# Weight-sum steps behind the MLP's tiles, two turns inside the embedding's products, and a shared last addition

## The chip, the cores and the metric

The kernel runs on one core of a Trainium2 chip. A core has several engines, each with its own instruction order that is fixed when the program is built: PE (TensorE, matrix products), DVE (VectorE), ACT (ScalarE), POOL (GpSimd) and SP (SyncE, which here issues most DMAs). An engine executes its instructions in that order; an instruction that waits for another engine or for a DMA holds up everything behind it on its engine. The metric is the device time of one execution in microseconds (us); lower is better.

## What is computed

The reference is a trunk of two layers over 512 tokens of width 1024. Each layer has a token mixer (Mamba-2 in the first, HGRN2 in the second), a layer norm, an MLP, a second layer norm and a gated embedding:

```python
h = layer_norm(DEEPNORM_ALPHA * x + mix, ln_g[i, 0], ln_b[i, 0])
h = layer_norm(DEEPNORM_ALPHA * h + sq_relu_mlp(h, mlp_w1[i], mlp_w2[i]), ln_g[i, 1], ln_b[i, 1])
x = h + jax.nn.sigmoid(h @ ple_w_gate[i]) * (p[i] @ ple_w_proj[i])

def sq_relu_mlp(h, w1, w2):
    a = jax.nn.relu(h @ w1)
    return (a * a) @ w2
```

All is float32. The MLP is 1024 to 4096 to 1024; `ple_w_gate` is 1024x1024 and `ple_w_proj` 256x1024.

## The kernel before

**Numbers in two halves.** A float32 operand is split into a high half (`hi`, a cast on ACT, L114 for weights) and a low half (`lo`, the difference on DVE, L116). A product is three matmuls, hi·hi, hi·lo and lo·hi, summed in a PSUM bank (`mm3`, L120 to L122). Weights stream in from memory through tiles `raw` or `r` and are split into tiles `whi` and `wlo`, six buffers of each, used again in turn.

**Seven products instead of eight.** Both the MLP's second product and the gate's product are done by 2x2 blocks with seven block products (Strassen-Winograd): p1 to p7. They need sums of blocks on both sides. On the activation side the blocks are named a11, a12, a22, s1, s2, s3, s4 (tiles `b8` and `blk`); on the weight side t1 to t4, made by `weight_sums`.

**The MLP** (`mlp_and_gate`) goes in four groups of 1024 hidden units. `hidden(g)` makes group g in eight tile steps ("T"): product, relu, square, and, after the fourth and the eighth, `half_blocks`, which forms one half of the seven blocks. Each block is written by `put`: a cast on ACT (L357), its difference on DVE (L358); the sums between them are L362 to L366. `block_product` multiplies the group by its part of w2 in seven steps ("Q"), one group behind. The order of steps is written out in `PERIODS`: eight T; then three times "TTQTQTQTQTQTQTQ"; then seven Q of the last group (g == 4), in the order p1, p7, p6, p4, p5, p2, p3. Each block product of 24 matmuls covers two halves c of 12 matmuls each, and the order of these on PE is the scheduler's. p1 and p6 share a pair of PSUM banks (`x`, tiles py0 and py1): p1's result must be added to `acc` (L471) before p6 adds more matmuls to the same bank and is added in its turn.

**Weight sums of the gate.** While the MLP runs, `sums_ahead` forms the gate's weight sums. For each of four pieces it loads four blocks into a `whi` and a `wlo` buffer (256 KB DMAs), does four additions (L405 to L410), and writes the four sums, twice two, each as a high half (cast L417 into `sg`, store L418) and a low half (difference L420 in place, store L425, both stores issued from ACT's queue) into the array `pre`. It is a generator of 20 steps, five for each piece; before the change one step is taken after each Q of the three mixed periods. What a step adds on DVE is placed behind the instruction in `marks["acc"]` (the last addition of a block product to `acc`), its low stores behind `marks["act"]` (the last relu).

**The gate and the embedding** follow. `turned(c)` transposes a 128-token row block of the normed `acc` on PE (L318, eight transposes into two banks, pt and pm), and ACT and DVE copy it out in halves (L308, L309) and whole (L324, L326). `proj(c, h)` is the embedding's product of six matmuls; `product` the gate's. turned(0) is issued in the MLP's last block product p3, after its last matmul; turned(1) between proj(0, 0) and proj(1, 0). `finish` multiplies the projection by the sigmoid (L611), adds it to `acc` (L612) and, in the last layer, stores it (L614). In the last layer's last call the projection comes in two halves of 256 columns.

The functions that the change touches, with the line numbers of the profile:

Of the kernel before, what the change touches and what calls it, by code (L numbers as in the profile page):

```python
# [11 lines left out]
AF = mybir.ActivationFunctionType  # L12
# [4 lines left out]
T = 512  # L17
# [15 lines left out]
SUMS = (60, 300, 300, 300)  # L33
# [8 lines left out]
def trunk(ctx: ExitStack, tc, a):  # L42
    nc = tc.nc
# [14 lines left out]
    uid, marks = [0], {}  # L58
# [8 lines left out]
    def f32(t):  # L67
        return t.bitcast(F32)
# [31 lines left out]
    def behind(ins):  # L100
        return nullcontext() if ins is None else tc.issue_after(ins.ins)
# [17 lines left out]
    def mm3(out, sh, sl, mh, ml, start, stop, **kw):  # L119
        nc.tensor.matmul(out, sh, mh, start=start, stop=False, **kw)  # L120
        nc.tensor.matmul(out, sh, ml, start=False, stop=False, **kw)  # L121
        marks["pe"] = nc.tensor.matmul(out, sl, mh, start=False, stop=stop, **kw)  # L122
# [25 lines left out]
    acc = mk(accp, [P, NCH, D], "acc")  # L148
# [10 lines left out]
    with tc.high_priority(offset=FIRST):  # L159
# [190 lines left out]
    def half_blocks(blk, z0, z1, p):  # L350

        ks = slice(2 * p, 2 * p + 2)
        a11, a12, a21, a22 = z0[:, :, 256:], z1[:, :, 256:], z0[:, :, :256], z1[:, :, :256]

        def put(name, f):
            hi, lo = blk[name][:, 0, ks, :], blk[name][:, 1, ks, :]
            nc.scalar.copy(hi, f)  # L357
            nc.vector.tensor_sub(lo, f, f32(hi))  # L358

        put("a11", a11)  # L360
        put("a22", a22)
        nc.vector.tensor_add(a22, a21, a22)  # L362
        put("a12", a12)
        nc.vector.tensor_sub(a21, a11, a21)
        nc.vector.tensor_sub(a11, a22, a11)
        nc.vector.tensor_sub(a12, a12, a11)  # L366
        put("s2", a11)
        put("s3", a21)
        put("s1", a22)
        put("s4", a12)  # L370
# [65 lines left out]
            us.append((hi, lo))  # L436
        return us

    def block_product(w, blk, lead, first, after=None, turns=None, sums=None):
# [8 lines left out]
        def product(x, f, name, start, i, j, turns=None):  # L448
            us = [split(v) if f in (t1, t2, t3, t4) else unit(v) for v in f]
            if start:  # L450
                banks[name] = [bank(psy, "py%d" % c) if name == "x" else bank(psj, "pj") for c in range(2)]
            t = blk[x]
            for c in range(2):
                ps = banks[name][c]
                sl = slice(c * P, (c + 1) * P)
                for k in range(4):
                    hi, lo = us[k // 2]
                    ks = slice((k % 2) * 512, (k % 2 + 1) * 512)
                    w_ = hi[:, ks], lo[:, ks]
                    mm3(ps, t[:, 0, k, sl], t[:, 1, k, sl], *w_, start and k == 0, k == 3, skip_group_check=True)  # L460
                    if turns and (c, k) == (1, 3):
                        with behind(marks["pe"]):
                            turns()
                d = acc[:, 2 - 2 * i + c, j * 512 : (j + 1) * 512]
                with tc.high_priority(offset=SOON if after else 0):
                    if after and f in (w[1][0], t1, t4, w[1][1]):
                        marks["acc"] = nc.vector.tensor_tensor_reduce(
                            d, ps, d, 1.0, 0.0, ALU.add, ALU.add, sums[:, 2 - 2 * i + c, j : j + 1]
                        )
                    elif (i, j) in seen:  # L470
                        marks["acc"] = nc.vector.tensor_add(d, ps, d)  # L471
# [10 lines left out]
        p3 = lambda: product("s4", w[1][1], "x", False, 0, 1, turns)  # L482
        for f in (p1, p7, p6, p4, p5, p2, p3) if after else (p1, p2, p6, p7, p5, p4, p3):
            f()
            if after and f is p5:
                after(0), after(1)
            if after and f is p3:
                after(2), after(3)
            yield

    def mlp_and_gate(layer, h_s, last, turns=()):

        w1, w2 = a[f"w1_{layer}"], a[f"w2_{layer}"]
        blocks = {}
# [45 lines left out]
        for g, period in enumerate(PERIODS):  # L540
            if g < 4:
                tiles = hidden(g)
            if g > 0:
                if g == 4:
                    blk, after, turned, sums, later = norm_blocks(2 * layer + 1)
                    p_s = (mk(w4, [P, 2, T], "a", F32R), mk(w4, [P, 2, T], "b", F32R))
                    praw = mk(raws, [P, 1024], "raw")
                    nc.sync.dma_start(praw, a[f"pT_{layer}"].rearrange("p k t -> p (k t)"))
                    praw = praw.rearrange("p (k t) -> p k t", k=2)
                    nc.scalar.copy(p_s[0], praw)  # L550
                    nc.vector.tensor_sub(p_s[1], praw, f32(p_s[0]))
                w = [[[w2[8 * g - 8 + 4 * i + 2 * j + u] for u in range(2)] for j in range(2)] for i in range(2)]
                products = block_product(w, blocks.pop(g - 1), SUMS[g - 1], g == 1, *((after, lambda: turned(0), sums) if g == 4 else ()))
            for op in period:
                next(tiles if op == "T" else products)
                if 0 < g < 4 and op == "Q":
                    next(ahead, None)
                if g == 4:
                    for _ in ahead:
                        pass  # L560
# [14 lines left out]

        pus, pps, held = {}, {}, {}

        def proj(c, h, parts=1):
            if h not in pus:
                pus[h] = unit(a[f"wp_{layer}"][h])  # L580
            pu = pus[h]
            pps[c, h] = []
            n = 512 // parts
            for i in range(parts):
                pp = bank(psj, "pj")[:, :n]
                for k in range(2):
                    ks = slice(k * 512 + i * n, k * 512 + (i + 1) * n)
                    mm3(pp, p_s[0][:, k, c * P : (c + 1) * P], p_s[1][:, k, c * P : (c + 1) * P], pu[0][:, ks], pu[1][:, ks], k == 0, k == 1)
                pps[c, h].append(pp)

        def product(x, f, c, ps, start, hook=()):
# [10 lines left out]
        def finish(c, h, sg):  # L602
            with behind(marks["pe"]):
                while late:
                    late.pop(0)()
            pp = pps.pop((c, h))
            n = 512 // len(pp)
            for i, part in enumerate(pp):
                cs = slice(i * n, (i + 1) * n)
                d = acc[:, c, h * 512 + i * n : h * 512 + (i + 1) * n]  # L610
                nc.vector.tensor_mul(sg[:, cs], part, sg[:, cs])  # L611
                nc.vector.tensor_add(d, sg[:, cs], d)  # L612
                if last:
                    nc.sync.dma_start(a["out"][c * P : (c + 1) * P, h * 512 + i * n : h * 512 + (i + 1) * n], d)  # L614
            if not last:
                late.append(lambda: turn(h, c))

        two = lambda p, tag: [bank(p, tag % c if "%" in tag else tag) for c in range(2)]
        proj(0, 0)
        with behind(marks["pe"]):  # L620
            turned(1)
        proj(1, 0)
        xb = two(psy, "py%d")
        f = [unit(v) for v in wb[0][0]]
        for c in range(2):
# [12 lines left out]
        f = ready(pre, 2)  # L638
# [9 lines left out]
        f = ready(pre, 1)  # L648
# [4 lines left out]
        f = ready(pre, 3)  # L653
# [14 lines left out]
        for c in range(2):  # L668
            if c == 0:
                proj(0, 1)  # L670
            product("s4", f, c, xb[c], False)
            sg = tmp("sg", [P, T])
            nc.scalar.activation(sg, xb[c], AF.Sigmoid)
            if c:
                proj(1, 1, 2 if last else 1)
            finish(c, 1, sg)
        return x_n, late

# [811 lines left out]
```

## Time and profile before

| | |
|---|---|
| time, median of 3 runs | 1411.1 us (1411.07 to 1411.56) |
| the profiled execution's own time | 1411.54 us |
| its span, first to last instruction | 1409.8 us |
| granted TensorE clock, mean | 1.000 |
| matmuls | 7973 |
| DVE busy | 1076.0 us (76%) |
| ACT busy | 777.6 us (55%) |

A row of the timeline has start, duration, engine, source line, operation, output<-input, and in brackets the idle time of the engine just before it with the releaser that the profile infers. "PE a L1 <- ACT b L2: 3.1, 2, 1.8" in the list of waits means that the line L1 on PE waited for L2 on ACT 3.1 us in total, in 2 places, 1.8 us at the longest. The releaser is inferred from the last semaphore event the profile can see, so it can name a neighbour of the real one. Matmuls overlap: a 128x512 matmul is listed with some 0.39 us, but they start 0.23 us apart.

### The profile page before, as it was taken

What the parts mean: (1) busy time and instruction counts of PE and PEld (TensorE: products, weight loads), DVE (VectorE), ACT (ScalarE), POOL (GpSimd) and SP (SyncE); (2) the same over time, 40 slices, a digit from 0 to 9 for tenths busy, and PEclk for the clock granted to TensorE, in tenths of its full rate; (3) what the DMA queues carried; (4) which work ended last, traced back from release to release, by engine and by line L of the source; (5) the groups of instructions that cost most, each with busy time, mean ns of one, the idle gap of its engine ahead of it and who ended that gap; (6) DMA issues with size and microseconds to landing.
All of it is one profiled execution on the core that took longest, in us unless ns stands there. A gap on an engine that the chain in (4) does not pass through costs nothing.

```text
span 1409.8 us, 20492 instructions
## 1 busy us (share of the span) xinstructions
PE 1400.4 (99%) x7973; PEld 1168.9 (83%) x7973; DVE 1076.0 (76%) x1777; ACT 777.6 (55%) x1164; POOL 1.8 (0%) x11
## 2 busy tenths in 40 slices
PE   9999999999999999999999999999999999999998
PEld 7888888888988888887888888888898888888787
DVE  7997877696866878787985774776785877868986
ACT  7886666573554555545564446465454554544563
POOL 0000000000000000000000000000000000000000
PEclk9999999999999999999999999999999999999999
DMA  8423333323354646655473321222163566565364
GB/s 295 157 98 135 103 108 120 105 90 105 129 185 143 228 161 204 211 176 177 139 280 122 104 92 62 89 92 75 61 239 122 171 209 214 175 215 194 108 246 154
DMA packets 66819, 214.70 MB, mean 152 GB/s; under 512 B 7713, under 2 KB 8353, under 8 KB 66593
## 3 DMA queue, kind: packets, MB, share of 16 engines
q1 hardware_dynamic: 57504, 196.59, 41.6%
q10 hardware_dynamic: 9216, 16.78, 3.3%
q8 instruction: 63, 1.03, 0.3%
q14 instruction: 36, 0.29, 0.1%
HBM read 194.41 MB, written 18.94 MB: 151 GB/s over the span
## 4 chain that ended last, share of the span: by engine, by line
PE 96%; DMA 1%; DVE 1%; ACT 1%; issue 1%; SPq 0%; DVEq 0%; ACTq 0%
PE pj L120 25%; PE pj L122 24%; PE pj L121 24%; PE py L120 5%; PE py L122 5%; PE py L121 5%; PE py L881 1%; PE py L1147 1%; PE py L883 1%; DVE wlo L116 1%; PE pt L864 0%; DMA raw<-in_whvg 0%; DMA acc<-in_xw 0%; ACT whi L114 0%; DMA pre<-whi 0%
## 5 line engine op out<-in xcount | busy, mean ns | idle before, releaser
L116 DVE TENSOR_TENSOR wlo<-raw,whi 128x1024 fp32r<-128x1024 f32 x222 | 269.4, 1221 | 171.6 <-ACT whi L114 170.4
L114 ACT CAST whi<-raw 128x1024 fp32r<-128x1024 f32 x222 | 232.8, 1051 | 302.3 <-PE pj L121 157.5
L120 PE MATMUL pj<-b,whi 128*128 128x512 f32 (+1 forms) x1000 | 379.6, 380 | 0.0
L121 PE MATMUL pj<-b,whi 128*128 128x512 f32 (+1 forms) x1000 | 377.3, 377 | 0.0
L122 PE MATMUL pj<-b,wlo 128*128 128x512 f32 (+1 forms) x1000 | 377.3, 377 | 0.0
L122 PEld LDWEIGHTS pj<-b,wlo 128*128 128x128 f32 x1000 | 188.2, 188 | 34.8
L121 PEld LDWEIGHTS pj<-b,whi 128*128 128x128 f32 x1000 | 188.2, 188 | 34.2
L120 PEld LDWEIGHTS pj<-b,whi 128*128 128x128 f32 x1000 | 188.0, 188 | 34.1
L122 PE MATMUL pj<-whi,b 128*128 128x512 f32 x530 | 206.1, 389 | 0.0
L120 PE MATMUL pj<-whi,b 128*128 128x512 f32 x496 | 196.1, 396 | 0.0
L121 PE MATMUL pj<-wlo,b 128*128 128x512 f32 x496 | 193.2, 390 | 0.0
L114 ACT CAST whi<-r 128x1024 fp32r<-128x1024 f32 x64 | 67.2, 1053 | 96.6 <-PE pj L121 79.9
L122 PEld LDWEIGHTS pj<-whi,b 128*128 128x128 f32 x530 | 99.5, 188 | 20.7 <-DVE b L1342 0.2
L120 PEld LDWEIGHTS pj<-whi,b 128*128 128x128 f32 x496 | 93.2, 188 | 20.3 <-ACT k L1076 0.5
L121 PEld LDWEIGHTS pj<-wlo,b 128*128 128x128 f32 x496 | 93.2, 188 | 18.5
L120 PE MATMUL py<-whi,b 128*128 128x512 f32 x256 | 100.7, 393 | 3.1 <-ACT b L357 3.1
L122 PE MATMUL py<-whi,b 128*128 128x512 f32 x256 | 99.8, 390 | 0.0
L121 PE MATMUL py<-wlo,b 128*128 128x512 f32 x256 | 99.7, 389 | 0.0
L116 DVE TENSOR_TENSOR wlo<-r,whi 128x1024 fp32r<-128x1024 f32 x64 | 77.8, 1220 | 27.8 <-ACT whi L114 24.0
L120 PEld LDWEIGHTS py<-whi,b 128*128 128x128 f32 x256 | 48.0, 188 | 15.0 <-ACT b L357 3.9
L122 PEld LDWEIGHTS py<-whi,b 128*128 128x128 f32 x256 | 48.1, 188 | 10.1
L121 PEld LDWEIGHTS py<-wlo,b 128*128 128x128 f32 x256 | 48.1, 188 | 9.7
(374 smaller groups left out, 1934.1 us busy)
## 6 DMA issues: line engine op xcount, KB each, us to landing
raw<-in_w SPq DMA_DIRECT2D x112, 512.0 KB, 3.4
r<-in_w SPq DMA_DIRECT2D x64, 512.0 KB, 4.0
raw<-in_wssd SPq DMA_DIRECT2D x38, 512.0 KB, 3.6
a<-csd SPq DMA_DIRECT2D x16, 512.0 KB, 3.6
raw<-in_wso SPq DMA_DIRECT2D x16, 512.0 KB, 3.7
pre<-sg ACTq DMA_DIRECT2D x32, 256.0 KB, 3.0
whi<-pre SPq DMA_DIRECT2D x16, 512.0 KB, 5.3
wlo<-pre SPq DMA_DIRECT2D x16, 512.0 KB, 6.6
```

The costliest lines, as they stand in the source:

```text
L114: nc.scalar.copy(hi[:, :n], f)
L116: nc.vector.tensor_sub(lo[:, :n], f, f32(hi[:, :n]))
L120: nc.tensor.matmul(out, sh, mh, start=start, stop=False, **kw)
L121: nc.tensor.matmul(out, sh, ml, start=False, stop=False, **kw)
L122: marks["pe"] = nc.tensor.matmul(out, sl, mh, start=False, stop=stop, **kw)
L881: nc.tensor.matmul(yd[64 * r : 64 * r + 64, sl], xdt[:, c, r, :], m[:, r, sl], start=True, stop=c == 0)
L883: nc.tensor.matmul(yd[64 * r : 64 * r + 64, sl], pv[:, c - 1, r, :], ecs[:, r, (c - 1) * P : c * P], start=False, stop=True,)
L1147: nc.tensor.matmul(ps[r][32 * b : 32 * b + 32, base + n * c : base + n * c + n], kk[r][:, ts], moving(r, 4 * c + b), start=True, stop=True,)
```

## The change

Four edits:

- `sums_ahead` is advanced after each T step of the mixed periods instead of each Q step, and `half_blocks`' differences (L358) now also set `marks["acc"]`, so a step's DVE work is placed behind the last of either kind.
- turned(0) goes from behind p3's last matmul to behind the third matmul of proj(0, 0), and turned(1) from between the two projections to behind the third matmul of proj(1, 0).
- The last sigmoid of the last layer is done in two halves of 256 columns.
- Where `finish` works in two halves (only that last call), the addition of the first half goes from DVE to GpSimd.

```diff
         def put(name, f):
...
-            nc.vector.tensor_sub(lo, f, f32(hi))
+            marks["acc"] = nc.vector.tensor_sub(lo, f, f32(hi))
...
-                    if turns and (c, k) == (1, 3):
-                        with behind(marks["pe"]):
-                            turns()
...
-                products = block_product(w, blocks.pop(g - 1), SUMS[g - 1], g == 1, *((after, lambda: turned(0), sums) if g == 4 else ()))
+                products = block_product(w, blocks.pop(g - 1), SUMS[g - 1], g == 1, *((after, sums) if g == 4 else ()))
             for op in period:
                 next(tiles if op == "T" else products)
-                if 0 < g < 4 and op == "Q":
+                if 0 < g < 4 and op == "T":
                     next(ahead, None)
...
+                    if turn == c and k == 0:
+                        with behind(marks["pe"]):
+                            turned(c)
...
-                nc.vector.tensor_add(d, sg[:, cs], d)
+                (nc.vector if i == len(pp) - 1 else nc.gpsimd).tensor_add(d, sg[:, cs], d)
...
-        proj(0, 0)
-        with behind(marks["pe"]):
-            turned(1)
-        proj(1, 0)
+        proj(0, 0, turn=0)
+        proj(1, 0, turn=1)
...
-            nc.scalar.activation(sg, xb[c], AF.Sigmoid)
+            parts = 2 if last and c else 1
+            for i in range(parts):
+                cs = slice(i * 512 // parts, (i + 1) * 512 // parts)
+                nc.scalar.activation(sg[:, cs], xb[c][:, cs], AF.Sigmoid)
             if c:
-                proj(1, 1, 2 if last else 1)
+                proj(1, 1, parts)
```

**Place 1: DVE at the hand-over from the fourth group to the last block product, first layer.** A row is line, operation, output<-input with the tiles' numbers, and size. L358 and L362 to L366 are the last call of `half_blocks`; L420 the last low halves of the sums; L471 (L468 in the changed file) the additions of block products to `acc`. wlo_946 is a half of t2, the weight of p6; py0_935 the bank that p1 and p6 share. Before:

```order
L420 TENSOR_TENSOR whi_859_5154<-whi_859_5154,sg_899_5462 128x512
L420 TENSOR_TENSOR wlo_860_5155<-wlo_860_5155,sg_900_5466 128x512
L116 TENSOR_TENSOR wlo_938_5642<-r_922_5578,whi_937_5640 128x1024
L471 TENSOR_TENSOR acc_1_94<-py0_842_5041,acc_1_94 128x512
L116 TENSOR_TENSOR wlo_940_5646<-r_925_5587,whi_939_5644 128x1024
L116 TENSOR_TENSOR wlo_944_5678<-r_923_5581,whi_943_5676 128x1024
L358 TENSOR_TENSOR blk_818_4938<-b_846_5079,blk_818_4938 128x512
L116 TENSOR_TENSOR wlo_946_5682<-r_926_5590,whi_945_5680 128x1024
L358 TENSOR_TENSOR b8_814_4934<-b_890_5393,b8_814_4934 128x512
L358 TENSOR_TENSOR b8_813_4933<-b_890_5393,b8_813_4933 128x512
L362 TENSOR_TENSOR b_890_5393<-a_869_5247,b_890_5393 128x2x256
L471 TENSOR_TENSOR acc_1_94<-py0_935_5612,acc_1_94 128x512
```

and with the change:

```order
L358 TENSOR_TENSOR blk_822_4956<-b_848_5091,blk_822_4956 128x512
L420 TENSOR_TENSOR whi_808_4906<-whi_808_4906,sg_867_5225 128x512
L420 TENSOR_TENSOR wlo_809_4907<-wlo_809_4907,sg_868_5229 128x512
L116 TENSOR_TENSOR wlo_944_5678<-r_923_5581,whi_943_5676 128x1024
L365 TENSOR_TENSOR a_873_5267<-b_892_5405,a_873_5267 128x2x256
L358 TENSOR_TENSOR blk_821_4955<-a_873_5267,blk_821_4955 128x512
L366 TENSOR_TENSOR b_892_5405<-b_892_5405,a_873_5267 128x2x256
L358 TENSOR_TENSOR b8_820_4954<-a_873_5267,b8_820_4954 128x512
L116 TENSOR_TENSOR wlo_946_5682<-r_926_5590,whi_945_5680 128x1024
L358 TENSOR_TENSOR b8_819_4953<-b_892_5405,b8_819_4953 128x512
L358 TENSOR_TENSOR blk_822_4956<-b_892_5405,blk_822_4956 128x512
L468 TENSOR_TENSOR acc_1_94<-py0_935_5612,acc_1_94 128x512
```

The two L420 stood ahead of the splits and of the half-block chain, and now stand inside that chain, ahead of p6's split wlo_946 and of the addition on py0_935. That addition followed L362; now eight half-block rows, three splits and the two L420 stand between, and two more splits (wlo_948, wlo_950) follow it, ahead of the addition on p1's other bank.

**The same place on ACT.** L528 is the relu, L530 the square, L425 the stores of the last low sums; with the change relu and square have just gone by. Before:

```order
L528 ACTIVATE b_890_5393<-pj_901_5470 128x512
L425 DMA pre_0<-whi_859_5154 128x512
L530 ACTIVATE b_890_5393<-b_890_5393 128x1024
L425 DMA pre_0<-wlo_860_5155 128x512
L114 CAST whi_939_5644<-r_925_5587 128x1024
L114 CAST whi_943_5676<-r_923_5581 128x1024
L357 CAST blk_818_4938<-b_846_5079 128x512
L114 CAST whi_945_5680<-r_926_5590 128x1024
L357 CAST b8_814_4934<-b_890_5393 128x512
L357 CAST b8_813_4933<-b_890_5393 128x512
```

and with the change:

```order
L357 CAST b8_818_4952<-b_892_5405 128x512
L357 CAST b8_817_4951<-b_892_5405 128x512
L114 CAST whi_939_5644<-r_925_5587 128x1024
L357 CAST b8_819_4953<-b_892_5405 128x512
L357 CAST blk_822_4956<-b_848_5091 128x512
L114 CAST whi_943_5676<-r_923_5581 128x1024
L357 CAST blk_821_4955<-a_873_5267 128x512
L425 DMA pre_0<-whi_808_4906 128x512
L425 DMA pre_0<-wlo_809_4907 128x512
L357 CAST b8_820_4954<-a_873_5267 128x512
L114 CAST whi_945_5680<-r_926_5590 128x1024
L357 CAST blk_822_4956<-b_892_5405 128x512
```

The stores stood ahead of the square and of all casts; they now stand behind the square and the casts of a22, a12, s1 and s3 (b8_818, b8_817, b8_819, blk_821), ahead of that of s2 (b8_820) and ahead of the cast for whi_945. The buffer read by the store "pre<-whi" was the one that whi_939 takes next; now it is the one that whi_945 takes.

**Place 2: PE at the two turns, first layer.** pj_1002 and pj_1005 are proj(0, 0) and proj(1, 0) before (pj_1000 and pj_1003 with the change), L318 the transposes. Before:

```order
L318 MATMUL pt_981_5883<-cst_17_160,acc_1_94 128x128 x4
L318 MATMUL pm_982_5884<-cst_17_160,acc_1_94 128x128 x4
L120 MATMUL pj_1002_5938<-whi_1000_5934,a_918_5570 128x512
L121 MATMUL pj_1002_5938<-wlo_1001_5936,a_918_5570 128x512
L122 MATMUL pj_1002_5938<-whi_1000_5934,b_919_5571 128x512
L120 MATMUL pj_1002_5938<-whi_1000_5934,a_918_5570 128x512
L121 MATMUL pj_1002_5938<-wlo_1001_5936,a_918_5570 128x512
L122 MATMUL pj_1002_5938<-whi_1000_5934,b_919_5571 128x512
L120 MATMUL pj_1005_5961<-whi_1000_5934,a_918_5570 128x512
L121 MATMUL pj_1005_5961<-wlo_1001_5936,a_918_5570 128x512
L122 MATMUL pj_1005_5961<-whi_1000_5934,b_919_5571 128x512
L318 MATMUL pt_1003_5945<-cst_17_160,acc_1_94 128x128 x4
```

and with the change:

```order
L120 MATMUL pj_1000_5922<-whi_998_5918,a_918_5570 128x512
L121 MATMUL pj_1000_5922<-wlo_999_5920,a_918_5570 128x512
L122 MATMUL pj_1000_5922<-whi_998_5918,b_919_5571 128x512
L318 MATMUL pt_1001_5926<-cst_17_160,acc_1_94 128x128 x4
L318 MATMUL pm_1002_5927<-cst_17_160,acc_1_94 128x128 x4
L120 MATMUL pj_1000_5922<-whi_998_5918,a_918_5570 128x512
L121 MATMUL pj_1000_5922<-wlo_999_5920,a_918_5570 128x512
L122 MATMUL pj_1000_5922<-whi_998_5918,b_919_5571 128x512
L120 MATMUL pj_1003_5945<-whi_998_5918,a_918_5570 128x512
L121 MATMUL pj_1003_5945<-wlo_999_5920,a_918_5570 128x512
L122 MATMUL pj_1003_5945<-whi_998_5918,b_919_5571 128x512
L120 MATMUL pj_1003_5945<-whi_998_5918,a_918_5570 128x512
```

turned(0), which stood in front of proj(0, 0), stands three matmuls into it; turned(1)'s first four transposes (pt), which stood three matmuls into proj(1, 0), follow its last matmul, three rows behind the last one shown.

On the g = 4 hand-over PE's order differs too: before, six of p6's matmuls stood between the two halves of p7; with the change all 24 matmuls of p7 come ahead of the first of p6. At the program's end GpSimd has two more rows, L612 ISA and L612 TENSOR_TENSOR (128x256), the first behind its last memset, and DVE's last three are L611, L611 and L612 instead of L611, L612, L611, L612.

More of the change, by code (lines that the diff above doesn't have):

```diff
@@ L437, in ready, with block_product @@
         return us
-    def block_product(w, blk, lead, first, after=None, turns=None, sums=None):
+    def block_product(w, blk, lead, first, after=None, sums=None):
         with behind(marks.pop(("turned", 0), None) if first else None):
@@ L446, in block_product, with product @@
         banks = {}
-        def product(x, f, name, start, i, j, turns=None):
+        def product(x, f, name, start, i, j):
             us = [split(v) if f in (t1, t2, t3, t4) else unit(v) for v in f]
@@ L481, in block_product @@
         p4 = lambda: product("a22", t4, "y", False, 1, 0)
-        p3 = lambda: product("s4", w[1][1], "x", False, 0, 1, turns)
+        p3 = lambda: product("s4", w[1][1], "x", False, 0, 1)
         for f in (p1, p7, p6, p4, p5, p2, p3) if after else (p1, p2, p6, p7, p5, p4, p3):
@@ L576, in mlp_and_gate, with proj @@
         pus, pps, held = {}, {}, {}
-        def proj(c, h, parts=1):
+        def proj(c, h, parts=1, turn=None):
             if h not in pus:
```

## The prediction

> **What bounds the kernel now.** I read the first and the fourth part of the page, then PE's waits, then the time around the longest of them on ACT, DVE and PE.
>
> ```profile
> span 1409.8 us, 20492 instructions
> PE 1400.4 (99%) x7973; PEld 1168.9 (83%) x7973; DVE 1076.0 (76%) x1777; ACT 777.6 (55%) x1164; POOL 1.8 (0%) x11
> PE 96%; DMA 1%; DVE 1%; ACT 1%; issue 1%; SPq 0%; DVEq 0%; ACTq 0%
> ...
> PE py L120 <- ACT b L357: 3.1, 2, 1.8
> PE pm L155 <- DVE y L152: 1.1, 1, 1.1
> PE py L120 <- ACT whi L174: 0.7, 2, 0.5
> PE pt L318 <- ACT b L324: 0.3, 1, 0.3
> ```
>
> PE is busy for 99% of the span, and the change takes no matmul away. So it can gain only the waits that it touches: 3.1 us at L357 (once in each layer), 0.3 us at L324, and what follows the last matmul. The L152 and L174 waits lie where nothing is edited. The profiled execution took 1411.54 us, 1.7 us more than its span and 0.44 us over the median 1411.1; I add differences to the median.
>
> The 3.1 us stand where the fourth MLP group hands over to the last block product. In the first layer, the order of the columns being start, duration, engine, line, operation:
>
> ```profile
> 654.14 0.69 DVE L420 TENSOR_TENSOR whi<-whi,sg 128x512 fp32r<-128x512 f32 x1
> 654.86 0.33 ACTq L425 DMA_DIRECT2D pre<-whi  x1
> 655.98 1.06 ACT L530 ACTIVATE b<-b 128x1024 f32<-128x1024 f32 x1
> 658.96 2.00 ACT L114 CAST whi<-r 128x1024 fp32r<-128x1024 f32 x2 [1.92 <-DMA pre<-whi]
> 662.33 1.14 ACT L357 CAST b<-b 128x512 fp32r<-128x512 f32 x2
> 665.26 0.68 DVE L362 TENSOR_TENSOR b<-a,b 128x512 f32<-128x512 f32 x1
> 665.87 0.68 DVE L471 TENSOR_TENSOR acc<-py,acc 128x512 f32<-128x512 f32 x1
> 665.08 0.39 PE L122 MATMUL pj<-whi,blk 128*128 128x512 f32 x1
> 666.70 0.47 PE L120 MATMUL py<-whi,b 128*128 128x512 f32 x1 [1.23 <-ACT b L357]
> ```
>
> The last pair of pieces of the weight sums (L420) is stored by a DMA issued at 654.86. The tile that this DMA reads is the next buffer for a weight split, so ACT's cast L114 stands until 658.96. Behind it in ACT's order stand the two half-block casts L357, whose input (the square, L530) was ready at 657.04 but which run at 662.33. DVE's halves follow, then L362, then the addition L471 that reads bank py0; it ends at 666.55, and PE's 666.70 starts s2 (p6) in that bank. The profile names ACT L357, but that had been done since 663.47: the last releaser is DVE's L471.
>
> **The change: sums.** Advanced after each tile step, the 20 steps end earlier in the program. That takes the DMA out from in front of that cast. But the last step comes behind the half-block lows (marks["acc"] is now set there too), and the orders of the change show where: DVE's two last L420 stand inside the last half-block chain, and ACT's L425 behind the casts of s1 and s3, ahead of the cast for whi_945. That cast refills the buffer which the DMA reads. On DVE the split of wlo_946 needs this cast, and the addition on py0_935, which p6 waits for, stands three rows behind this split. The wait for the landing is moved, not removed.
>
> I work the queue out by hand, from rows of before. First the anchors and the pitches:
>
> ```profile
> 658.28 0.39 PE L122 MATMUL py<-whi,blk 128*128 128x512 f32 x1
> 659.87 0.39 PE L120 MATMUL py<-whi,b 128*128 128x512 f32 x1
> 662.59 0.39 PE L120 MATMUL pj<-whi,blk 128*128 128x512 f32 x1
> 672.55 0.50 PE L120 MATMUL py<-whi,b 128*128 128x512 f32 x1
> ...
> 660.04 2.36 DVE L116 TENSOR_TENSOR wlo<-r,whi 128x1024 fp32r<-128x1024 f32 x2 [2.00 <-PE py L122]
> 664.06 1.29 DVE L358 TENSOR_TENSOR b<-b,b 128x512 fp32r<-128x512 f32 x2
> ...
> 1307.44 4.07 DMA pre<-whi
> pre<-whi ACTq DMA_DIRECT2D x16, 256.0 KB, 3.8
> ```
>
> Twelve matmuls take 662.59 − 659.87 = 2.72 us. On DVE one 128x512 operation follows another after 0.60 us and lasts 0.69 (L358 x2: 1.29, each 0.69 long). Two L116 take 2.36, so the next operation follows one after some 1.13, by the same overlap of 0.09. Two of ACT's big casts take 2.00, one alone 1.05 (as at 1307.93 below, of the same size).
>
> - ACT: the square ends at 657.04, the two casts L357 at 658.2. The cast for whi_939 needs the matmul of 658.28 done: 658.71 to 659.76. So the two casts do come five microseconds sooner than the 662.33 of before.
> - DVE from 659.80 in its new order: L116 to 660.93, L364, L358 at 661.53, L420 at 662.13 to 662.82, L420 at 662.73, L116 at 663.33, L365 at 664.46, L358 at 665.06, L366 at 665.67, L358 at 666.27 to 666.95.
> - The store is issued when the first L420 ends, 662.85. With 3.8 us (the median of its 16) it lands at 666.65. ACT casts whi_945 until 667.70; DVE's L116 starts at 667.74, two L358 at 668.87 and 669.47, and the addition on py0_935 runs 670.07 to 670.75. p6 can start at 670.80.
> - PE, in its new order, runs all 24 matmuls of p7 first, so it gets to p6 at 662.59 + 5.44 = 668.03. It stands 2.77 us there. Then 12 matmuls, and the next bank's addition behind two more L116 (670.67 + 2.26 + 0.69 = 673.62): p1's second half starts at 673.65.
>
> In both kernels the same 48 matmuls lie between 659.87 and p1's second half, and without a wait it would start at 670.75. Before started it at 672.55, so 1.80 us were lost; now 2.90. Layer 0: **+1.1 us**.
>
> The second layer repeats this, 651.95 us later by its first p1 matmul and its square:
>
> ```profile
> 1307.93 1.06 ACT L530 ACTIVATE b<-b 128x1024 f32<-128x1024 f32 x1
> 1311.82 0.39 PE L120 MATMUL py<-whi,b 128*128 128x512 f32 x1
> 1319.27 0.47 PE L120 MATMUL py<-whi,b 128*128 128x512 f32 x1 [1.84 <-ACT b L357]
> 1325.12 0.50 PE L120 MATMUL py<-whi,b 128*128 128x512 f32 x1
> ```
>
> Here 1325.12 − (1311.82 + 10.88) = 2.42 us were lost before; with the same 2.90 now, **+0.5 us**. Together +1.6.
>
> The landing time is the unknown. From 666.87 − 1.05 − 662.85 = 2.97 us downwards it no longer matters, for DVE then gets to this L116 at 666.87 anyway, and the addition ends at 669.88: 0.87 us less in each layer, a sum of −0.2. Each microsecond of landing above 3.8 costs one in each layer: at the 4.07 of the chain's row +2.1. I take 3.8, since it is the same transfer.
>
> [...]
>
> In groups one to three the sums steps come behind tile steps instead of products. PE's order there is unchanged, and its waits above name nothing of those groups; the same DVE and ACT operations are only moved between products. I take 0. If that cover failed, a late split would cost one DVE operation of 0.6 to 1.2 us per place; DVE at 76% of the span leaves room for that.
>
> **The two turns.** Transposes of turned(0) and turned(1) go three matmuls (0.68 us) later. Around the second turn, before:
>
> ```profile
> 701.92 1.05 ACT L114 CAST whi<-raw 128x1024 fp32r<-128x1024 f32 x1 [0.58 <-DMA raw<-in_wg]
> 702.88 0.58 ACT L324 COPY b<-pt 128x512 f32<-128x512 f32 x1
> 702.85 0.40 PE L122 MATMUL pj<-whi,b 128*128 128x512 f32 x1
> 703.51 0.66 PE L318 MATMUL pt<-cst,acc 128*128 128x128 f32 x4 [0.26 <-ACT b L324]
> ```
>
> PE could have begun at 702.85 + 0.23 = 703.08 and began at 703.51, when L324 had emptied bank pt. L324 ran behind the cast of 701.92, which waited for a load and not for the turn. If cast and copy stay there, PE now asks at 703.76 and finds the bank free: −0.43. If all of it shifts with the transposes, 0. I take **−0.3**, nearer the first, as the cast's load has no tie to the turn. The second layer has no such wait.
>
> **The tail.** Columns as above:
>
> ```profile
> 1404.75 0.28 PE L122 MATMUL pj<-whi,b 128*128 128x256 f32 x1
> ...
> 1405.47 0.28 PE L122 MATMUL pj<-whi,b 128*128 128x256 f32 x1
> 1405.14 0.42 DVE L611 TENSOR_TENSOR sg<-pj,sg 128x256 f32<-128x256 f32 x1 [1.46 <-PE pj L122]
> 1405.95 0.42 DVE L611 TENSOR_TENSOR sg<-pj,sg 128x256 f32<-128x256 f32 x1
> 1406.40 0.43 DVE L612 TENSOR_TENSOR acc<-sg,acc 128x256 f32<-128x256 f32 x1
> 1404.36 0.60 ACT L673 ACTIVATE sg<-py 128x512 f32<-128x512 f32 x1 [2.12 <-PE py L122]
> 729.09 0.99 POOL L1009 MEMSET sc<- 128x512 f32 x2 [387.66 <-DVE b L309]
> ```
>
> The sigmoid ends at 1404.96, before DVE's first product at 1405.14, which waited for PE; its halves gain nothing. Without the first addition DVE's second product starts when PE's last matmul is out, 1405.47 + 0.28 + 0.11 = 1405.86 instead of 1405.95; 0.11 is how far the first product came behind the matmul of 1404.75. So the last addition ends 0.09 us sooner: **−0.1**. GpSimd's addition starts at 1405.6. The nearest rows are DVE's 0.43 for that addition and POOL's own memset, 0.5 for twice the elements. Its store is queued on SP ahead of the last one, which is ready at 1406.74; so up to about 0.8 us it costs nothing, and beyond that each tenth costs a tenth. [...]
>
> Sum: 1.6 − 0.3 − 0.1 = +1.2; 1411.1 + 1.2 = **1412.3 us**.
>
> **Rivals.** (a) The wait goes away: 1.80 + 2.42 + 0.4 + 0.1 = 4.7 us, 1406.4. For it: casts that were ready at 657.04 ran at 662.33, and now run at once. Against it: 13 DVE rows stand from the split of wlo_940 to p6's addition, three L116 and ten shorter, 9.4 us of work from 659.80, and PE is there at 668.03. It decides if DVE in fact takes that addition earlier than its order says; I give it 0.14. (b) The store lands within 3 us: fewer loads run at 662 than at 654. Then −0.2 − 0.4, 1410.5; 0.24. (c) Slower, by the same store: it lands as late as 5.3 us, as whi<-pre does at its median (twice the bytes), and every microsecond over 3.8 is paid twice, 1415.3; from 4.6 us upwards it is over the bound. 0.17.
>
> ```profile
> whi<-pre SPq DMA_DIRECT2D x16, 512.0 KB, 5.3
> ```
>
> [...] No row shows a load here, and its row in the order waits for nothing; 0.05.
>
> **How the numbers follow.** The forecast has 0.40, with its own range 1411.3 to 1413.9 from landings of 3.3 to 4.6. Differences under 0.2% (2.8 us) are about what a measurement of this kernel cannot tell from none. Faster than 1408.3 is (a) with a little of (b): 0.16. Slower than 1413.9 is most of (c), half of (d), and an edge of the forecast: 0.24. The rest, 0.60, is the same. The range 1408.5 to 1415.0 leaves out (a) and the far ends of (c) and (d).
>
> **What would show it.** In the profile after: PE's longest wait in each layer sits some 36 matmuls after p1 begins, 1.9 to 3.5 us, put down to DVE or to ACT's L358 chain; a cast L114 idle "<-DMA pre<-whi" ahead of it; DVE's L420 just before it. If that cast has no idle time before it, (b) holds; if p6 starts within 0.5 us of p7's end, (a) does and my hand-made queue is wrong. L324's wait should be gone, and POOL's addition last under 0.8 us.

## The result and the profile after

| | before | with the change |
|---|---|---|
| median, 12 executions each | 1411.78 us | 1415.56 us |
| lowest to highest | 1410.95 to 1414.12 | 1413.95 to 1418.44 |
| profiled execution, time / span | 1411.54 / 1409.8 us | 1414.55 / 1412.6 us |
| mean granted clock, profiled execution | 1.000 | 0.999 |

The ratio is 1.0027, 95% interval 1.0019 to 1.0035: the change makes the kernel slower by 0.27%. The prediction had 1412.3 us with no measurable difference as the likeliest, and a range of 1408.5 to 1415.0.

From the page of the changed kernel (its head, part 1 and part 4):

```profile
span 1412.6 us, 20506 instructions
PE 1401.3 (99%) x7973; PEld 1171.2 (83%) x7973; DVE 1076.6 (76%) x1776; ACT 775.5 (55%) x1165; POOL 2.5 (0%) x12
PE 98%; DVE 1%; DMA 1%; ACT 0%; issue 0%; DVEq 0%; ACTq 0%
```

And its list of PE's waits (total, times, longest):

```profile
PE py L120 <- DVE acc L468: 6.1, 2, 3.1
PE pm L155 <- DVE y L152: 1.1, 1, 1.1
```

The two waits of 1.2 and 1.8 us at L357 have become two of 3.0 and 3.1 us, now put down to the instruction that really releases them, the addition to `acc` (L468 here). The waits at L324 and L570 are gone.

The hand-over in the first layer, from the timeline, first DVE and ACT, then PE:

```profile
661.79 0.69 DVE L420 TENSOR_TENSOR whi<-whi,sg 128x512 fp32r<-128x512 f32 x1
662.51 0.33 ACTq L425 DMA_DIRECT2D pre<-whi  x1
666.87 1.05 ACT L114 CAST whi<-r 128x1024 fp32r<-128x1024 f32 x1 [1.39 <-DMA pre<-whi]
667.95 1.22 DVE L116 TENSOR_TENSOR wlo<-r,whi 128x1024 fp32r<-128x1024 f32 x1 [1.32 <-ACT whi L114]
670.29 0.68 DVE L468 TENSOR_TENSOR acc<-py,acc 128x512 f32<-128x512 f32 x1
...
659.52 0.39 PE L120 MATMUL py<-whi,b 128*128 128x512 f32 x1
671.03 0.50 PE L120 MATMUL py<-whi,b 128*128 128x512 f32 x1 [3.00 <-DVE acc L468]
673.90 0.50 PE L120 MATMUL py<-whi,b 128*128 128x512 f32 x1
```

The chain of waits has the store's way to its landing as a piece of its own (start, length):

```profile
662.51 4.28 DMA pre<-whi
```

The store is issued when the first L420 has ended, and the cast that refills its buffer stands until it has landed, 4.28 us later. While it is under way the DMA engines are busy, as PE's view over the two stores' flights shows (after length, PE's busy time and granted clock: the DMA engines' mean busy share, and GB/s):

```profile
662.51:666.79 4.28, 4.28 (x20) 1.00 0.76 244
1315.30:1319.75 4.45, 4.45 (x20) 1.00 0.79 234
```

These are about 1.04 MB in each: this store and the other low store with 256 KB each, and a load of 512 KB (`b<-in_ln`, issued at 661.90 in the first layer). Everything behind follows at DVE's pitch. From p1's first matmul (659.52) to p1's second half (673.90) it takes 14.38 us, where 48 matmuls need 10.88: 3.50 us are lost, 1.80 before.

The second layer does the same, and then something more:

```profile
1315.30 0.33 ACTq L425 DMA_DIRECT2D pre<-whi  x1
1319.78 1.05 ACT L114 CAST whi<-r 128x1024 fp32r<-128x1024 f32 x1 [1.51 <-DMA pre<-whi]
...
1312.31 0.39 PE L120 MATMUL py<-whi,b 128*128 128x512 f32 x1
1323.95 0.50 PE L120 MATMUL py<-whi,b 128*128 128x512 f32 x1 [3.12 <-DVE acc L468]
1324.29 0.39 PE L121 MATMUL py<-wlo,b 128*128 128x512 f32 x1
1324.86 0.63 PE L120 MATMUL py<-whi,b 128*128 128x512 f32 x1
1325.29 0.63 PE L121 MATMUL py<-wlo,b 128*128 128x512 f32 x1
...
1327.42 0.63 PE L120 MATMUL py<-whi,b 128*128 128x512 f32 x1
1328.39 0.40 PE L120 MATMUL py<-whi,b 128*128 128x512 f32 x1
```

From 1324.86 to 1327.42 seven matmuls last 0.63 us instead of 0.39 and start 0.43 us apart instead of 0.23. The granted clock says why. The view of PE by stretches (length, busy time and count, granted clock, share and rate of DMA) for the two hand-overs, from p1's first matmul to its second half:

```profile
659.52:673.90 14.38, 11.38 (x49) 1.00 0.23 73
1312.31:1328.39 16.08, 12.96 (x49) 0.89 0.22 66
```

Between 1325.29 and 1327.85 alone it is 0.50. Before, the clock was 1.00 in both hand-overs. The 16.08 us are 5.20 lost, against 2.42 before; 7 × 0.20 = 1.4 of them are the slow matmuls.

Followed from one kernel to the other, the same instruction stands at −0.35 us when p1 begins (659.87 and 659.52; this execution had a quicker start, which is not of the change), at +1.35 at p1's second half, at +0.49 when the second layer's p1 begins, at +3.27 at its second half, and at +2.83 at the last matmul (1405.47 and 1408.30). So the hand-overs cost 1.70 and 2.78 us, and between and behind them 0.86 and 0.44 come back.

The tail of the changed kernel, on PE, POOL and DVE:

```profile
1408.30 0.28 PE L122 MATMUL pj<-whi,b 128*128 128x256 f32 x1
1408.47 0.72 POOL L612 TENSOR_TENSOR acc<-sg,acc 128x256 f32<-128x256 f32 x1 [678.21 <-DVE sg L611]
1409.14 0.42 DVE L612 TENSOR_TENSOR acc<-sg,acc 128x256 f32<-128x256 f32 x1
```

GpSimd's addition takes 0.72 us and ends before DVE's. The L612 ISA of its order has no row in the timeline; POOL's row ahead of the addition is a memset at 730.14, 0.12 us long. The last addition ends 1.26 us after the last matmul starts, 1.36 before.

### The profile page after: what moved, and what is told of

It reads as the page before. It is cut to its first block, busy times and chain, and to the rows that moved or that the text cites. A ratio compares the mean times of both kernels' runs of the same rounds, so it can differ in the third digit from the quotient of the medians.

```text
span 1412.6 us, 20506 instructions
## 1 busy us (share of the span) xinstructions
PE 1401.3 (99%) x7973; PEld 1171.2 (83%) x7973; DVE 1076.6 (76%) x1776; ACT 775.5 (55%) x1165; POOL 2.5 (0%) x12
## 4 chain that ended last, share of the span: by engine, by line
PE 98%; DVE 1%; DMA 1%; ACT 0%; issue 0%; DVEq 0%; ACTq 0%
PE pj L120 25%; PE pj L121 24%; PE pj L122 24%; PE py L120 5%; PE py L122 5%; PE py L121 5%; PE py L882 1%; PE py L1148 1%; PE py L884 1%; DMA pre<-whi 1%; PE pt L865 0%; PE pt L226 0%; PE pm L155 0%; DVE b L358 0%; PE pt L825 0%; PE pt L1317 0%
```

## The experiments

Theory A is the prediction's mechanism with one term added that the trace after suggests: PE's long standstill is followed by a lower granted clock (behind 3.12 us, 0.50 from 1325.29 to 1327.85). The rivals are B (turns, or GpSimd's addition, cost the time), C (the sums steps cost PE time among the tiles), and D (the late DVE queue alone, without the clock). Times are medians; each is compared with the kernel before on the same chip. The changed kernel's 1415.56 comes from other executions, so differences against it are good to about a microsecond.

| kernel | time | before, same chip | ratio, 95% interval | granted clock of its executions |
|---|---|---|---|---|
| sums edit alone | 1416.83 | 1412.55 | 1.0026 (1.0017 to 1.0035) | 0.994 to 0.999 |
| turns and tail alone | 1412.22 | 1412.55 | 0.9999 (0.9990 to 1.0008) | 0.996 to 1.000 |
| all, steps ended earlier | 1405.11 | 1412.55 | 0.9947 (0.9934 to 0.9959) | 1.000 |
| all, addition ahead of the split | 1416.14 | 1412.55 | 1.0027 (1.0018 to 1.0036) | 0.995 to 0.999 |
| all but the new mark | 1405.07 | 1412.13 | 0.9952 (0.9940 to 0.9965) | 0.999 to 1.000 |
| early steps, no turns, no tail | 1405.15 | 1412.13 | 0.9952 (0.9940 to 0.9965) | 0.999 to 1.000 |
| all, last two stores left out | 1410.05 | 1412.13 | 0.9985 (0.9977 to 0.9994) | 0.999 to 1.000 |
| early steps and turns, no tail | 1405.56 | 1412.13 | 0.9953 (0.9939 to 0.9967) | 1.000 |
| steps behind T alone | 1405.53 | 1412.48 | 0.9945 (0.9931 to 0.9959) | 0.999 to 1.000 |
| new mark alone | 1412.28 | 1412.48 | 0.9995 (0.9986 to 1.0004) | 0.998 to 1.000 |

### Sums alone, and all but the sums

The kernel before with

```diff
-            nc.vector.tensor_sub(lo, f, f32(hi))
+            marks["acc"] = nc.vector.tensor_sub(lo, f, f32(hi))
...
-                if 0 < g < 4 and op == "Q":
+                if 0 < g < 4 and op == "T":
```

> The kernel before with the sums edit alone (steps behind T, L358 sets the mark); turns and tail as before. Theory A (the sums edit moves the wait for the store's landing to whi_945, PE stands 3.1 us before p6 in each layer, and an idle time that long lowers the granted clock for some 3 us): slower than the kernel before by the changed kernel's 3.8 us plus the 0.9 that turns and tail had gained there, about +4.7 us, PE's longest waits 3.0 to 3.3 us in both layers, mean clock under 1.000. Theory B (turns or GpSimd's addition cost the time): within 1 us of the kernel before.

It is 4.3 us slower than the kernel before, as slow as the whole change. Its waits:

```profile
PE py L120 <- DVE acc L471: 6.1, 2, 3.1
```

And PE over stretches that begin just ahead of each standstill, the fourth number being the granted clock:

```profile
668.00:677.00 9.00, 5.92 (x19) 0.81 0.00 0
1322.20:1332.00 9.80, 6.80 (x17) 0.65 0.07 21
```

Here the clock fell after both standstills. The sums edit carries the loss. The changed kernel with these two lines undone:

> The changed kernel with the sums edit undone: only turns, sigmoid halves and GpSimd's addition. Theory A: 0.4 (turn at L324) to 0.9 us (also L570's wait, and the tail) faster than the kernel before, waits at L357 of 1.2 and 1.8 us as before, clock 1.000. Theory B: 2 us or more slower than the kernel before.

It measures the same as the kernel before, so B is out; a gain of 0.4 to 0.9 us can be neither shown nor excluded with this interval. The rest of the expectation was a miss: the waits at L357 are not 1.2 and 1.8 us but 2.2 and 2.5, and the clock was 0.996 to 1.000. The list of waits has no L324. The waits:

```profile
PE py L120 <- ACT b L357: 4.7, 2, 2.5
```

PE's timeline behind the first of them:

```profile
666.73 0.77 PE L120 MATMUL py<-whi,b 128*128 128x512 f32 x1 [2.19 <-ACT b L357]
667.29 0.63 PE L121 MATMUL py<-wlo,b 128*128 128x512 f32 x1
```

And the stretches around both:

```profile
664.10:671.00 6.90, 4.71 (x14) 0.75 0.21 72
1317.20:1324.20 7.00, 4.53 (x20) 1.00 0.22 77
```

A standstill of 2.2 us was followed by a fall of the clock, one of 2.5 us was not.

### Where the last step stands

The changed kernel, with two steps at each of the first two T of the first two mixed periods, so that the last step comes four T earlier:

```diff
-            for op in period:
+            for n, op in enumerate(period):
...
                 if 0 < g < 4 and op == "T":
                     next(ahead, None)
+                    if g < 3 and n < 2:
+                        next(ahead, None)
```

> The changed kernel with two sums steps at each of the first two T of the first two mixed periods, so that the last step comes four T earlier and the last store lies ahead of the last half-block chain. By the order DVE then has no L420 and no landing wait ahead of the addition on py0_935. Theory A: no wait ahead of p6 worth naming (under 0.4 us), the 1.8 and 2.4 us that the kernel before lost there and 0.9 of turns and tail gained: about 5 us faster than the kernel before, 1406.9, clock 1.000. Theory C (moving sums steps among the tiles of the groups costs PE time in itself): not faster than the kernel before, with new waits between 400 and 650 us.

It is 7.4 us faster than the kernel before on that chip, and faster than the changed one by 10; 1406.9 was expected, and the further 1.8 us were not traced. PE has no wait left but one at the program's start:

```profile
PE pm L155 <- DVE y L152: 1.1, 1, 1.1
```

The addition on py0, the first of these two, starts at 666.25 and is out before p6's first matmul (timeline):

```profile
666.25 1.28 DVE L468 TENSOR_TENSOR acc<-py,acc 128x512 f32<-128x512 f32 x2
667.49 0.62 PE L120 MATMUL py<-whi,b 128*128 128x512 f32 x2
```

In the second layer's hand-over PE is busy all the time, at full clock:

```profile
1300.00:1330.00 30.00, 30.00 (x133) 1.00 0.22 76
```

C is out: the tiles bear the steps at no cost. Which of the two sums lines does the harm? Undoing only the mark in `half_blocks` (the three `behind(marks["acc"])` in `sums_ahead` become `behind(marks.get("acc"))`, since the first step now comes ahead of any addition):

```diff
-            marks["acc"] = nc.vector.tensor_sub(lo, f, f32(hi))
+            nc.vector.tensor_sub(lo, f, f32(hi))
```

> The changed kernel with one line of the sums edit undone: steps still behind T, but the half-block differences (L358) no longer set the mark, so a step's DVE work is placed behind the last addition to acc only (behind nothing for the steps ahead of the first one). By the order the two last L420 then stand ahead of the last half-block chain. Theory A (what costs is where the last L420 and its store land, not that the steps moved to T): no wait ahead of p6 over 0.4 us, 1405 us, as the kernel with the early steps (1405.1). Theory C (steps behind T cost by themselves): within 2 us of the changed kernel, 1414 to 1418.

1405.07 us: one line makes 10 us of difference to the changed kernel. The view of L420 by tile shows that the last of the first layer's now starts at 609, not at 662, so its store has long landed:

```profile
L420 DVE TENSOR_TENSOR whi<-whi,sg x3: 684/685/685, 560.5 to 609.0; 128x512 fp32r<-128x512 f32 x3
```

The kernel before with each line by itself. Steps behind T, the mark as it was:

> The kernel before with one change: the sums steps behind T instead of Q, the mark as before (set by the additions to acc only). If the whole gain of the early kernels lies in the step's place and not in turns, tail or the mark: 1405.1 +- 0.5, no wait ahead of p6, clock 0.999 to 1.000 in every execution. If turns and tail are needed for part of it: 1406 or more.

1405.53 us and no wait at the hand-overs. (Here too the three `behind` take `marks.get("acc")`.) And the mark alone, with the steps behind Q:

> The kernel before with the other half alone: the half-block differences (L358) set the mark, the steps stay behind Q. By the order nothing moves at the hand-over (the two L420 go one row ahead), so the waits at L357 stay, 1.2 to 2.5 us: within 1 us of the kernel before, its clock 0.996 to 1.000. If setting the mark were harmful by itself: 2 us or more slower.

Nothing moves, as its waits show:

```profile
PE py L120 <- ACT b L357: 3.2, 2, 1.6
PE pm L155 <- DVE y L152: 1.1, 1, 1.1
PE pt L318 <- ACT b L324: 0.3, 1, 0.3
```

So the steps behind T are the gain, the mark alone is neutral, and together they lose: the mark ties the last step to a half-block low (s4 of the first half, blk_822 in DVE's order with the change). In the changed kernel's first layer ACT's cast for this block starts at 660.05, PE's last matmul that reads a `blk` tile in that period at 659.29, and the low and the two L420 follow on DVE. That this matmul is what keeps the block back is read from the times, not tested.

### The landing itself

The changed kernel without its last two low stores; the high halves are written in their place, so a quarter of two weight sums has a wrong low half:

```diff
                         nc.scalar.dma_start(dst[n, u, 0][:, cs], f32(hi))
+                        final = u == h == 1 and pair[0][0] == 0
+                        if final:
+                            nc.scalar.dma_start(dst[n, u, 1][:, cs], f32(hi))
...
                         for to, x in lows:
-                            nc.scalar.dma_start(to, x)
+                            if not final:
+                                nc.scalar.dma_start(to, x)
```

> The changed kernel without its last two low stores: that piece of the low halves in memory is given the high halves instead, from the cast's own tile, so a quarter of two weight sums is wrong in its low half; no instruction waits for the landing of the last L425 stores. The L420 stay inside the half-block chain. Theory A (the landing wait): the cast for whi_945 has no DMA ahead of it, p1's second half starts some 1.4 us sooner in each layer, PE's idle time breaks into about 1.1 us inside p7 and 0.8 us ahead of p6, and with it the falls of the clock go: 2.9 us from the waits and 1 to 3 from the clock, 1410 to 1412 where the changed kernel has 1415.6. Rival (the two L420 in DVE's queue cost the time, not the landing): within 1 us of the changed kernel.

1410.05 us, 5.5 less than the changed kernel. The standstill falls into two short ones in each layer (waits):

```profile
PE py L120 <- DVE acc L472: 1.8, 2, 0.9
PE pj L122 <- DVE blk L358: 1.2, 2, 0.6
```

So the landing, with what it does to the clock, is worth 5.5 of the 10.5 us that separate the changed kernel from the early ones. Of the other 5.0 these four waits, which the two L420 and the rest of DVE's queue leave, make 3.0; the rest was not traced. (The wait inside p7 was expected at 1.1 and is 0.6.)

### One standstill or two

The changed kernel with p1's additions at a higher priority in the scheduler, so that the first stands ahead of the split wlo_946 on DVE:

```diff
-                with tc.high_priority(offset=SOON if after else 0):
+                with tc.high_priority(offset=300 if after and x == "a11" else SOON if after else 0):
                     if after and f in (w[1][0], t1, t4, w[1][1]):
```

> The changed kernel with p1's additions (L468) at a higher priority in the scheduler: the addition on py0_935 now stands right behind the two L420 on DVE, ahead of the split wlo_946. The wait for the store's landing stays, and so does the addition on p1's other bank, behind the splits. So PE's 3.1 us in one piece should break into two, some 1.3 us ahead of p6 and some 1.7 us ahead of p1's second half, whose start (14.0 us after p1's first matmul) hardly moves. Theory A: no idle time over 3 us, so no fall of the clock: 1.5 to 3 us faster than the changed kernel, clock 1.000. Theory D (the time is the late DVE queue alone, the clock plays no part): as slow as the changed kernel, within 0.5 us.

It was meant to split the standstill and so to tell A from D. It does not: p6 starts with hardly a wait, and the whole 2.9 us stand ahead of p1's second half, whose addition is still behind the splits. The waits:

```profile
PE py L120 <- DVE acc L468: 5.8, 2, 2.9
```

PE's timeline in the first layer:

```profile
674.33 0.80 PE L120 MATMUL py<-whi,b 128*128 128x512 f32 x1 [2.88 <-DVE acc L468]
674.92 0.63 PE L121 MATMUL py<-wlo,b 128*128 128x512 f32 x1
```

And the stretches from ahead of both standstills:

```profile
671.00:678.00 7.00, 4.12 (x11) 0.76 0.12 40
1325.40:1333.40 8.00, 5.12 (x16) 0.79 0.20 66
```

The clock fell after both, and the time is that of the changed kernel. The expectation of 1.3 + 1.7 us was a miss; the run tells nothing between A and D, but adds two falls to the count.

What tells A from D is the count over all executions. The six kernels whose traces have no standstill over 1.1 us at the hand-overs, or none at all, hold a clock of 0.999 or 1.000: those with early or unmarked steps in 25 executions, the one without the last stores in 11. The changed kernel, the sums alone and the addition ahead, with standstills of 2.9 to 3.1 us, have 0.994 to 0.999 in 33 executions: 23 of these lie below 0.999, and none of the other 36. A mean of 0.999 by itself says little, for it also counts the time behind the last matmul, where a fall costs nothing. So it is in the trace of the steps behind T alone (the last 4.0 us, no matmul left, clock 0.64):

```profile
1401.30:1405.30 4.00, 0.00 (x0) 0.64 0.19 60
```

Within the changed kernel the span goes with the clock: 1412.8 us on average at 0.999 (7 executions), 1414.1 at 0.997 (3), 1415.6 and 1416.0 at 0.996 and 0.994. Cut into stretches of 10 us up to 1400 us, the twelve traces have a clock under 1.00 only at the hand-overs of these three kernels and of turns and tail alone. That the standstill brings the fall is shown by this, by the counts and by the kernels that remove it; how the chip decides when to fall is not.

### Turns and tail, where the clock is steady

The kernel before with the sums edit and the early steps, turns and tail as before:

> The kernel before with the sums edit and the two double steps alone; turns and tail as before. Against the kernel with all edits and double steps (1405.1) this prices turns and tail where nothing disturbs the clock. By my sum of 0.3 (L324) to 0.8 us (also L570's wait) for the turns and 0.1 for the tail: 1405.5 to 1406.0. If turns and tail were worth nothing: 1405.1.

1405.15 us against 1405.11 with turns and tail, on two chips on which the kernel before differs by 0.4: they are worth nothing that shows. For the turns, the trace tells why. With the turns where they were, ACT and PE around the second turn:

```profile
698.70 1.05 ACT L114 CAST whi<-raw 128x1024 fp32r<-128x1024 f32 x1 [0.17 <-DMA raw<-in_wg]
699.65 0.58 ACT L324 COPY b<-pt 128x512 f32<-128x512 f32 x1
...
700.28 0.66 PE L318 MATMUL pt<-cst,acc 128*128 128x128 f32 x4
```

The cast ahead of L324 waits 0.17 us for its load instead of 0.58, L324 ends at 700.23, and PE's transposes follow at 700.28, without an entry for L324 in the list of waits. The load comes earlier against the cast. This goes with the steps behind T, not with the length of the hand-over: in the sums alone, which stand 3.1 us there and leave the turns where they were, the same cast has no wait for its load and L324 none in PE's list, while the new mark alone, with the steps behind Q, keeps the 0.3 us. The cast in the sums alone:

```profile
704.50 1.05 ACT L114 CAST whi<-raw 128x1024 fp32r<-128x1024 f32 x1
```

How the steps bring the load forward was not traced. And the early steps with the turns, but without sigmoid halves and GpSimd's addition:

> The kernel with the early sums steps and the turns, without sigmoid halves and GpSimd's addition. Tail worth 0.1 us by my sum: 1405.2 against the 1405.1 with all. If GpSimd's addition (0.72 us in the changed kernel's trace) costs anything on the store's queue, this is 0.2 us or more faster than 1405.1.

1405.56, 0.4 more than the 1405.11 with both, within the spread of the fast kernels' executions (1404.6 to 1407.1): neither the 0.1 gain nor a cost of the addition on GpSimd can be told.

## Why the prediction was wrong, point by point

The path was right, and every sign that the prediction named for it is in the trace. Two terms of the sum failed: a standstill of PE was priced at its own length, without what the clock adds, and the store's landing was put too short.

- **What bounds the kernel, and who releases p6.** Right. The addition on py0 is now named by the profile itself, and removing the wait for the store removes the loss.
- **The wait is moved, not removed; DVE's new order.** Right to a few hundredths: the store was forecast 2.98 us after p1's first matmul (662.85 against 659.87) and came 2.99 after it. Rival (a), that the wait goes away, did not happen.
- **The landing time.** Mis-sized. I took 3.8 us, the median of 16; from issue to the cast it was 4.36 in the first layer (4.28 to the landing) and 4.48 in the second. By the prediction's own rule, a microsecond for a microsecond, that is +0.6 and +0.7. With these the forecast would have been 1413.6, still inside the range. Taking the median over all 16 stores was the mistake; the chain's row for this very store, 4.07, was nearer and stood beside it. Rival (b) counted on fewer loads at the later time, but the change moved the traffic along with the store: the DMA engines were 0.76 and 0.79 busy during its flight, against 0.83 and 0.84 before (and 0.33 before in the stretch from 662.51 to 666.79). That this traffic set the landing time was not tested.
- **What a standstill costs.** This step failed. The sum priced PE's 2.77 us at 2.77 us. In the profiled execution the second one brought 1.4 us more by the clock, and executions with a lower mean clock had spans up to 3.4 us longer. No term and no rival had it: the trace of before had clocks of 1.00 around its standstills of 1.2 and 1.8 us, and said nothing on longer ones. In the traces of the experiments and of the change, six of the eight standstills of 2.2 to 3.1 us were followed by a fall, in the changed kernel's second layer to 0.50, with 0.43 us between matmuls against 0.23.
- **The turns, −0.3.** Counted where it was not left to gain. Turns and tail alone have no wait at L324, as forecast; but the steps behind T remove it too, with the turns where they were. With both edits the turns add nothing that shows.
- **The tail, −0.1.** 0.1 in the trace, in no time that could show it. GpSimd's 0.72 us lies inside the cover of 0.8, and its addition ends ahead of DVE's: no later end by GpSimd (rival (d), 0.05) shows.
- **Groups one to three, 0.** Nearly. PE's list has no wait there; the shift that PE gathers between the two hand-overs was not followed row by row.
- **The sum.** With the landings measured and one fall of the clock, the terms are 1.6 + 1.3 + 1.4 − 0.4 = +3.9, where the medians differ by 3.8. The 4.3 of the hand-overs are close to the 4.48 followed in the trace. The −0.4 is not what came back (1.30, and 0.35 at the start), and the falls differ between executions, so that the closeness of the total is partly luck. The forecast also started from 1411.1, the median of three executions; that of twelve is 1411.78, and these 0.7 us are not the change's.
- **What can be told apart.** Set too coarse. The sum took differences under 2.8 us for none; the interval of the ratio is 0.08% wide to each side, some 1.1 us.

## What to carry to other kernels

A wait that one edit removes can stand up again where the same edit puts the waiting work: ask of each moved store which buffer it holds and who needs that buffer next, and of each position ("behind this instruction") what that instruction itself must wait for. Price a standstill of the matrix engine of two or three microseconds above its own length, because a lower clock may follow it: here one followed six of the eight traced ones of 2.2 to 3.1 us. Look at what else is on the DMA engines while a store is under way: here they were 0.76 and 0.79 busy, and whether that set its landing time was not tested. One of two lines gained 7 us alone and lost 4 with the other, so parts of an edit are worth running one at a time.

## What the runs showed of the hardware

- The granted clock fell behind a standstill of 2.2 us (1 of 1 traced), not behind one of 2.5, and behind five of six of 2.9 to 3.1 us; in the changed kernel it was 0.50 from 1325.29 to 1327.85. The slow phase lasted seven matmuls (3.0 us) in the changed kernel's second layer and 5.5 us in that of the sums alone:

```profile
1326.26 0.63 PE L121 MATMUL py<-wlo,b 128*128 128x512 f32 x1
...
1331.38 0.56 PE L121 MATMUL py<-wlo,b 128*128 128x512 f32 x1
```

- A 256 KB store from ACT's queue took 4.36 and 4.48 us before its buffer could be used again, with the DMA engines 0.76 and 0.79 busy during its flight (the shares of 0.23 and 0.22 in the rows of the hand-overs are over stretches of 14 to 16 us).
- The kernel before loses clock too: beside the experiments its mean clock was 1.000 in 17 of 56 executions, with a mean span of 1409.7 us, and 0.997 in four, with 1412.9. Its waits at L357, 1.2 and 1.8 us in its own trace, are 1.6 and 1.6 in that of the new mark alone and 2.2 and 2.5 in that of turns and tail alone, the two other kernels that keep them. In which of its executions the clock fell at the hand-overs was not traced.
- The fastest kernels here, 1405.1 us, are 0.5% faster than the kernel before. What the hand-overs lost and the waits at L324 and L570 account for 1.8 + 2.4 + 0.3 + 0.2 = 4.7 of some 7 us; part of the rest may be the clock of the kernel before. It was not traced.
